# A hybrid encoder block on one core: the right-hand SBUF pools begin 96 bytes lower

## The chip, the cores and the metric

The kernel runs on one core of one Trainium2 chip. The metric is the device time in microseconds of one execution. Three runs of the kernel before took 1058.28, 1058.58 and 1059.94 us; the median is 1058.58 us. A profile of one execution goes with it.

## The reference

The reference is one encoder block over T = 1040 positions (16 meta tokens put ahead of 1024) of 1024 channels, in float32.

```python
u = _rms_norm(h, pre_w)
z = u @ w_in                       # ten parts: 1024 x 7680
# branch A: bidirectional retention, 4 heads (dk 128, dv 256), chunks of 128
o_r = group_norm(retention_fwd + retention_bwd) * ret_nw * silu(rg)
y_r = o_r @ w_rb
# branch B: attention within +-128, 8 query heads, 2 key groups, meta keys, a sink logit
o_a = windowed_sink_attention(aq, ak, av, sink) * silu(ag)
y_a = o_a @ w_ab
mix = sigmoid(gr) * y_r + sigmoid(ga) * y_a
return h + _rms_norm(mix @ w_o, post_w)
```

(The middle lines are shortened; rotary positions and the decay tables are left out here.)

## The kernel before

The products need more than one rounded pass. Each operand is split into a high part (a copy rounded to the matmul's type, on ScalarE or GpSimd) and a low part (the difference, on VectorE, L89 to L90), and `mm3` (L72 to L78) issues three matmuls for one product of tiles:

```python
nc.tensor.matmul(o, ah, bh, start=first, stop=False, **kw)   # L74
nc.tensor.matmul(o, al, bh, start=False, stop=False, **kw)   # L75
latest[:] = [nc.tensor.matmul(o, ah, bl, start=False, stop=last, **kw).ins]   # L76
```

The second argument is the stationary operand, which a weight load brings into the array (128 x 128); the third is the moving operand, which is streamed past it (256 to 512 columns). Each matmul has its own weight load.

Tiles live in pools. A pool on the left grows up from the low end of each partition, one with `side="right"` grows down from the high end. The right-hand pools are `wp` (L46: the split weights `wh` and `wl` of a unit of 256 columns, and the packed meta tokens `xm`), `aw` (L1331: split queries `aqh` and `aql`, the raw scores) and, when these two are closed (L1529), `lp` (L1530: split blocks `lh` and `ll`, six of each, raw weights, staging tiles). The left-hand ones that matter are `keep` (L44: `big`, the split input in four tiles of 4 x 1040 columns, and small vectors such as `nsink`, `dtab`, `rcol`, `rbc`, `rnw`, `mhalf`, L93 to L99), `ra`, `rp`, `va`, `ap` (retention and attention) and `yt` (L1546: the tiles T2, T3 and T4).

The built program shows where the tiles begin in each partition. The right-hand pools end at byte 229,344; `wp` begins at 194,528 and `lp` at 172,000, both 224 modulo 256. Every stationary tile in them has rows of 512 bytes or a multiple, so all of them begin at 224 modulo 256. In `big` a row of 1040 columns is 4160 bytes, so each step of the contraction index k moves the address by 64 bytes modulo 256: the slices pass through 0, 64, 128 and 192. The slices of T in `yt` all begin at 64 modulo 256, the retention's split tiles in `rp` and `va` at 192.

The work has three stages.

- Projections, retention and attention (0 to about 560 us). `proj` (L135) makes transposed projections: the stationary operand is a weight from `wp`, the moving one a slice of `big` (256, 272 or 512 columns). `projT` (L155) makes the values (`pv`, `pav`) the other way round: the stationary operand is a slice of `big`, the moving one 256 columns of `wp`. Retention (L440) multiplies tiles of `rp` with tiles of `rp`; attention (L1337) takes its queries from `aw`. Projections of the next head fill the gaps of retention and attention in a hand-written order.
- The gates and the two branch projections (to about 975 us), and the output projection (to the end). They are done in 2 x 2 blocks with seven products in place of eight (`Phase`, L931 on). `product` (L987) issues four `mm3` per product: the stationary operand is `lh` or `ll` from `lp`, the moving one 512 columns of `big` or T. Blocks are prepared six products ahead (`LEAD`, L1080).

The order of the instructions on each engine comes from this hand-written order and a scheduler.

Of the kernel before, what the change touches and what calls it, by code (L numbers as in the profile page):

```python
# [7 lines left out]
F32 = mybir.dt.float32  # L8
# [8 lines left out]
P = 128  # L17
# [21 lines left out]
def block_kernel(ctx: ExitStack, tc: tile.TileContext, x0, xT, x, meta, w_in, w_rb, w_ab, w_out, post_w,  # L39
# [2 lines left out]
    PSUM = bass.MemoryType.PSUM  # L42

    keep = ctx.enter_context(tc.tile_pool(name="keep", bufs=1))  # L44
    w_stack = ExitStack()
    wp = w_stack.enter_context(tc.tile_pool(name="wp", bufs=1, side="right"))  # L46
    ps = ctx.enter_context(tc.tile_pool(name="ps", bufs=1, reuse_waits="tile", space=PSUM))
# [43 lines left out]


    vec = keep.tile([P, 2 * KT], F32, name="vec")  # L93
    nsink = keep.tile([P, 8], F32, name="nsink")
    dtab = keep.tile([P, 28], F32, name="dtab")
    rcol = keep.tile([P, 9], F32, name="rcol")
    rbc = keep.tile([P, T], F32, name="rbc")
    rnw = keep.tile([P, KT], F32, name="rnw")
    mhalf = keep.tile([P, 16], F32, name="mhalf")  # L99
    nc.vector.memset(mhalf, -0.5)  # L100

    def fetch_w(src, u):
# [163 lines left out]
    with tc.tile_pool(name="setup", bufs=1, reuse_waits="tile") as st:  # L266
# [89 lines left out]
        for c in range(9):  # L356
            a, b = cols(c)
            t = st.tile([P, D if c < 7 else T], F32, tag="xn" if c < 7 else "xr", bufs=7 if c < 7 else KT - 1,
                        name=f"xn{c}")[:, 0:D]
# [1271 lines left out]
```

## Time and profile before

| what | value |
|---|---|
| median of three runs | 1058.58 us (1058.28 to 1059.94) |
| span of the profiled execution | 1057.8 us |
| TensorE busy | 1047.6 us, 99% |
| weight loads | 906.6 us, 86%, beside the matmuls |
| VectorE busy | 839.3 us, 79% |
| ScalarE busy | 507.2 us, 48% |
| GpSimd busy | 229.0 us, 22% |
| granted TensorE clock | 0.999 of full speed |
| read from and written to HBM | 124.32 MB and 57.68 MB |

A row of a group of instructions gives the source line, the engine, what is written from what, the shape, the count, and then busy time in us, the mean duration in ns, and the engine's idle time before it. The duration of a matmul overlaps that of the next one, since matmuls are pipelined; what counts for the time is the distance from one start to the next, and that is read from the timeline, whose rows begin with the start in us. A row of waits gives the engine that waited, the line, what it waited for, the total in us, how often, and the longest. A row of windows gives the stretch, its length, each engine's busy time with its count, PEclk, the DMA share and GB/s; with a filter, it gives PE's alone.

### The profile page before, as it was taken

How to read it: one execution, taken by the hardware profiler on the slowest of the kernel's cores; microseconds unless marked ns; L12 is line 12 of the kernel's file. 1: busy time of each engine (PE TensorE's matmuls, PEld its weight loads, DVE VectorE, ACT ScalarE, POOL GpSimd, SP SyncE). 2: the span in 40 equal slices, each digit the busy share in tenths (PEclk: the TensorE clock that was granted, in tenths of full speed). 3: DMA queues.
4: the chain of work that ended last, by engine and by line, in shares of the span. 5: the costliest groups of instructions: out<-in, count | busy, mean ns of one | idle time of the engine just before them, and what ended most of it. 6: DMA issues, size and time to landing. Idle time of an engine off the chain costs nothing. (4 is left out here: it accounts for less than half of the span.)

```text
span 1057.8 us, 17223 instructions
## 1 busy us (share of the span) xinstructions
PE 1047.6 (99%) x5880; PEld 906.6 (86%) x5880; DVE 839.3 (79%) x1788; ACT 507.2 (48%) x1127; POOL 229.0 (22%) x338
## 2 busy tenths in 40 slices
PE   9999999999999999999999999999999999999997
PEld 8998999989989888988888888787888888788886
DVE  7876758768875777778769988998799799778665
ACT  5531422523524566655667554455556446334432
POOL 3345244243242332444310000000000000111032
PEclk9999999999999999999999999999999999999999
DMA  9433222242231466665549679999925746789463
GB/s 352 168 86 86 70 42 80 71 98 89 84 83 61 101 181 192 165 181 159 165 155 338 201 254 321 302 309 353 387 94 168 250 159 232 225 226 317 119 120 79
DMA packets 96758, 188.43 MB, mean 178 GB/s; under 512 B 10944, under 2 KB 35552, under 8 KB 95856
## 3 DMA queue, kind: packets, MB, share of 16 engines
q1 hardware_dynamic: 79120, 162.89, 45.6%
q0 software_dynamic: 10176, 14.73, 9.2%
q10 hardware_dynamic: 7376, 9.73, 2.6%
q8 instruction: 46, 0.75, 0.3%
q14 instruction: 40, 0.33, 0.1%
HBM read 124.32 MB, written 57.68 MB: 172 GB/s over the span
## 5 line engine op out<-in xcount | busy, mean ns | idle before, releaser
L1246 POOL DMA_DIRECT2D mx_d<-c1a x4 | 3.6, 891 | 401.6 <-DVE c1a L1237 382.4
L75 PE MATMUL bz<-T,llz 128*128 128x512 f32 x192 | 75.9, 395 | 0.0
L76 PE MATMUL bz<-T,lhz 128*128 128x512 f32 x192 | 75.7, 394 | 0.0
L74 PE MATMUL bz<-T,lhz 128*128 128x512 f32 x192 | 75.6, 396 | 0.0
L74 PE MATMUL pv<-wh,big 128*128 128x256 f32 x256 | 73.3, 286 | 0.0
L75 PE MATMUL pv<-wh,big 128*128 128x256 f32 x256 | 73.3, 286 | 0.0
L76 PE MATMUL pv<-wl,big 128*128 128x256 f32 x256 | 73.2, 286 | 0.0
L75 PE MATMUL bz<-big,llz 128*128 128x512 f32 x176 | 69.6, 395 | 0.2 <-DVE llz L90 0.2
L76 PE MATMUL bz<-big,lhz 128*128 128x512 f32 x176 | 69.5, 395 | 0.0
L74 PE MATMUL bz<-big,lhz 128*128 128x512 f32 x176 | 68.7, 395 | 0.5 <-ACT lhz L942 0.5
L1377 ACT ACTIVATE p<-raw,nm 128x401 f32<-128x401 f32 (+1 forms) x64 | 38.4, 601 | 33.7 <-DVE nm L1374 32.4
L1387 POOL TENSOR_SCALAR p<-p,den 128x400 f32<-128x400 f32 (+1 forms) x60 | 37.8, 687 | 68.2 <-DVE den L1380 64.1
L74 PE MATMUL paq<-big,wh 128*128 128x512 f32 x128 | 51.8, 405 | 0.0
L75 PE MATMUL paq<-big,wl 128*128 128x512 f32 x128 | 50.7, 396 | 0.0
L76 PE MATMUL paq<-big,wh 128*128 128x512 f32 x128 | 50.5, 395 | 0.0
L75 PEld LDWEIGHTS pv<-wh,big 128*128 128x128 f32 x256 | 48.3, 189 | 0.4
L74 PEld LDWEIGHTS pv<-wh,big 128*128 128x128 f32 x256 | 48.2, 188 | 0.4
L76 PEld LDWEIGHTS pv<-wl,big 128*128 128x128 f32 x256 | 48.3, 189 | 0.3
L76 PEld LDWEIGHTS bz<-T,lhz 128*128 128x128 f32 x192 | 36.0, 188 | 8.9
L75 PEld LDWEIGHTS bz<-T,llz 128*128 128x128 f32 x192 | 36.0, 188 | 8.8 <-DVE llz L90 0.3
L74 PEld LDWEIGHTS bz<-T,lhz 128*128 128x128 f32 x192 | 36.0, 188 | 8.7
L90 DVE TENSOR_TENSOR wl<-wr,wh 128x1024 fp32r<-128x1024 f32 x28 | 34.8, 1247 | 10.8 <-POOL wh L87 6.7
(616 smaller groups left out, 3613.6 us busy)
## 6 DMA issues: line engine op xcount, KB each, us to landing
wrz<-in_w_in_dram SPq DMA_DIRECT2D x32, 512.0 KB, 6.2
wr<-in_w_in_dram SPq DMA_DIRECT2D x29, 512.0 KB, 4.0
we<-in_w_in_dram SPq DMA_DIRECT2D x16, 512.0 KB, 4.2
tg<-tg_d SPq DMA_DIRECT2D x32, 256.0 KB, 5.0
T<-preT SPq DMA_DIRECT2D x6, 1024.0 KB, 8.2
e<-e ACTq DMA_DIRECT2D x20, 256.0 KB, 2.6
e<-e SPq DMA_DIRECT2D x20, 256.0 KB, 4.6
xn<-in_x_dram SPq DMA_DIRECT2D x8, 512.0 KB, 9.2
```

Of the source, the lines that this page charges most:

```text
L74: nc.tensor.matmul(o, ah, bh, start=first, stop=False, **kw)
L75: nc.tensor.matmul(o, al, bh, start=False, stop=False, **kw)
L76: latest[:] = [nc.tensor.matmul(o, ah, bl, start=False, stop=last, **kw).ins]
L90: return nc.vector.tensor_tensor(o, i, hi.bitcast(F32), ALU.subtract).ins
L1246: nc.gpsimd.dma_start(d, to, accum_op=ALU.add)
L1377: last["exp"] = nc.scalar.activation(p[:, 0:1 + wid], raw[e_][:, 0:1 + wid], AF.Exp, scale=-1.0, bias=nm_[:, e_:e_ + 1], accum_out=den[:, ...
L1387: nc.gpsimd.tensor_scalar(pt[e_][:, 0:wid], pt[e_][:, 0:wid], den[:, e_:e_ + 1], 1.0, op0=ALU.mult, op1=ALU.mult)
```

## The change

A pool `edge` is opened on the right ahead of `wp`, with one tile of 24 columns (96 bytes), of which 8 hold `nsink`, formerly in `keep`. `mhalf` grows from 16 to 24 columns, so that `keep` has the size it had.

```diff
     keep = ctx.enter_context(tc.tile_pool(name="keep", bufs=1))
+    edge = ctx.enter_context(tc.tile_pool(name="edge", bufs=1, side="right"))
     w_stack = ExitStack()
     wp = w_stack.enter_context(tc.tile_pool(name="wp", bufs=1, side="right"))
...
-    nsink = keep.tile([P, 8], F32, name="nsink")
+    nsink = edge.tile([P, 24], F32, name="nsink")[:, 0:8]
     dtab = keep.tile([P, 28], F32, name="dtab")
     rcol = keep.tile([P, 9], F32, name="rcol")
     rbc = keep.tile([P, T], F32, name="rbc")
     rnw = keep.tile([P, KT], F32, name="rnw")
-    mhalf = keep.tile([P, 16], F32, name="mhalf")
+    mhalf = keep.tile([P, 24], F32, name="mhalf")
     nc.vector.memset(mhalf, -0.5)
```

In the built program every tile of `wp`, `aw` and `lp` begins 96 bytes lower: 128 modulo 256 in place of 224. `dtab`, `rcol`, `rbc`, `rnw` and `mhalf` begin 32 bytes lower. All other tiles stay. Source lines from L45 on are one higher in the kernel after.

## The prediction

> **What bounds the kernel now.** I read the page's first part, then the engine's waits, then a table by window, and last the timeline of single matmuls.
>
> ```profile
> span 1057.8 us, 17223 instructions
> PE 1047.6 (99%) x5880; PEld 906.6 (86%) x5880; DVE 839.3 (79%) x1788; ACT 507.2 (48%) x1127; POOL 229.0 (22%) x338
> ```
>
> TensorE is busy for all but 10.2 us of the span. The waits of PE alone:
>
> ```profile
> PE idle L309 <- DVE warm L207: 1.5, 1, 1.5
> PE bz L74 <- ACT lhz L942: 0.5, 1, 0.5
> PE pt L1404 <- POOL p L1387: 0.5, 2, 0.3
> PE pt L1404 <- DVE pal L90: 0.4, 1, 0.4
> PE pt L1409 <- DVE pbl L90: 0.3, 1, 0.3
> PE bz L75 <- DVE llz L90: 0.2, 1, 0.2
> ```
>
> Together 3.4 us. So the time is the sum of the distances from one matmul's start to the next, plus a start and a tail that the edit does not lengthen. The windows say that the clock is not a variable here:
>
> ```profile
> 100.00:200.00 100.00, 100.00 (x778) 95.97 (x777) 74.71 (x212) 34.52 (x106) 36.22 (x56) 1.00 0.24 64
> 800.00:900.00 100.00, 100.00 (x431) 80.49 (x430) 92.75 (x154) 53.66 (x97) 0.00 (x0) 1.00 0.64 213
> ```
>
> PEclk is 1.00 in both, and between 800 and 900 us 431 matmuls fill 100 us, 232 ns each. A change of addresses can only matter by moving that distance. How many matmuls read an operand from the moved side? The windows filtered by tile, over the whole span, first for matmuls that read T, then for those that read big:
>
> ```profile
> 0.00:1057.80 1057.80, 244.29 (x1020) 1.00 0.58 178
> 0.00:1057.80 1057.80, 679.21 (x3456) 1.00 0.58 178
> ```
>
> These 4476 of 5880 matmuls, 923.5 us of busy time, each pair one left-hand operand (T or big) with one right-hand operand. I therefore watch 0.2% of the whole, 2.1 us: that is about 0.5 ns per matmul of this group, and about what a measurement of this kernel can tell from no change.
>
> **What the change does to the instructions.** From the two built programs: all five queues hold the same instructions in the same order with the same waits; only the memset of mhalf is wider. Every tile of wp, aw and lp begins 96 bytes lower, so 224 modulo 256 becomes 128; five small tiles of keep begin 32 bytes lower; nothing else moves. So no wait is added, removed or passed, and no DMA is issued anywhere else.
>
> The memset:
>
> ```profile
> 0.80 0.07 DVE L100 MEMSET mhalf<- 128x16 f32 x1 [0.80 <-PEq L1621]
> 1.37 0.06 DVE L207 MEMSET warm<- 128x1 f32 x1
> ```
>
> 16 columns take 70 ns and 1 column 60, so 8 more columns cost about 5 ns, ahead of the first matmul's 1.5 us wait: +0.005 us, on the path, nothing.
>
> The other engines read and write moved tiles as well. A subtraction that touches lp alone or with keep, one that reads left tiles and writes keep's big, and one that writes yt:
>
> ```profile
> L90 DVE TENSOR_TENSOR llz<-wrz,lhz 128x512 fp32r<-128x512 f32 x36 | 24.4, 692 | 4.3 <-ACT lhz L942 4.2
> L90 DVE TENSOR_TENSOR big<-z,big 128x512 fp32r<-128x512 f32 x16 | 10.9, 694 | 0.0
> L90 DVE TENSOR_TENSOR T<-xT,T 128x512 fp32r<-128x512 f32 x12 | 7.7, 688 | 0.0
> ```
>
> Tiles at 224 (llz, lhz), at 0, 64, 128 and 192 (big, 4160-byte rows, so each k begins 64 bytes further) and at 64 (T) take 688 to 694 ns. I cost VectorE's and ScalarE's work at no change. The cover, if they did move, is the 3.4 us of waits above: PE hardly ever waits for them. DMAs go to the same tiles at other offsets; no PE wait in the list names one, so I cost them at nothing too.
>
> **The weight loads.** Four kinds of stationary operand: big at all four phases against a right-hand moving operand (pv), lhz at 224 against T at 64, val in ra at 192, vh in rp at 192 (the last two not on the right):
>
> ```profile
> L74 PEld LDWEIGHTS pv<-wh,big 128*128 128x128 f32 x256 | 48.2, 188 | 0.4
> L74 PEld LDWEIGHTS bz<-T,lhz 128*128 128x128 f32 x192 | 36.0, 188 | 8.7
> L75 PEld LDWEIGHTS po<-pah,val 128*128 128x128 f32 x64 | 12.1, 189 | 1.1
> L74 PEld LDWEIGHTS pa<-vh,sh 128*128 128x128 f32 x32 | 6.0, 189 | 0.3
> ```
>
> 188 to 189 ns whether the tile begins at 224, 192, or one of 0, 64, 128, 192. big already serves as stationary operand at 128 for a quarter of its loads and is no cheaper. So a stationary address of 128 modulo 256 buys nothing in the load by itself: bound 0 to 1 ns per load, and it lies beside the running matmul.
>
> **The distance between matmuls.** This is the term with something in it. First and last of 60 starts that stream T, of 70 that stream big, of 48 pv, and of 12 in a row with both operands in rp:
>
> ```profile
> 641.82 0.39 PE L74 MATMUL bz<-T,lhz 128*128 128x512 f32 x1
> 655.82 0.39 PE L74 MATMUL bz<-big,lhz 128*128 128x512 f32 x1
> ...
> 889.22 0.39 PE L74 MATMUL br<-big,lhr 128*128 128x512 f32 x1
> 905.50 0.40 PE L74 MATMUL ba<-T,lha 128*128 128x512 f32 x1
> ...
> 36.91 0.28 PE L75 MATMUL pv<-wh,big 128*128 128x256 f32 x1
> 42.56 0.28 PE L75 MATMUL pv<-wh,big 128*128 128x256 f32 x1
> ...
> 214.36 0.28 PE L74 MATMUL pa<-vh,sh 128*128 128x256 f32 x1
> 215.79 0.28 PE L76 MATMUL pk<-big,wh 128*128 128x256 f32 x1
> ```
>
> - T: 14.00 us / 60 = 233.3 ns. Both addresses are fixed modulo 256: moving 64, stationary 224.
> - big: 16.28 / 70 = 232.6 ns. Stationary 224, moving walking through four phases.
> - pv: 5.65 / 48 = 117.7 ns. Moving 224, stationary walking through four phases.
> - rp: 1.43 / 12 = 119.2 ns. Both at 192, the same stretch of columns as pv.
>
> So the distance depends on the pair of addresses, but little: 0.7 ns of 233 (0.3%) and 1.5 ns of 118 (1.3%). Where one operand walks, all four differences are passed through, and it is a little quicker; where the pair is fixed, it is a little slower. After the change big still walks through four differences, now multiples of 64 bytes in place of odd multiples of 32, and T has one fixed pair again (64 against 128). An average over four evenly spaced differences should stay where it is; the fixed pair may stay at 233.3 or fall to the walking 232.6. The value I take for big is 0, bounds below; for T, between 0 and 0.7 ns on 996 matmuls (0.7 us), I take half, -0.3 us. (The 996 are the 1020 of the windows row less the 24 half-width ones of the last product.)
>
> **Sum.** 1057.8 us span + 0.005 (memset) + 0 (other engines) + 0 (loads) + 0 (big) - 0.3 (T) = 1057.5 us. The runs' median, 1058.58 us, lies 0.8 us above the span of the profiled execution, which I keep: 1058.3 us.
>
> **Rivals.**
>
> - *Slower: the aligned pace.* The only stretches in which both operands stand on one 64-byte grid without a right-hand tile are those like rp's, and they are the slow ones, 119.2 against 117.7. If the pace is set by whether the two reads stand on the same 64-byte grid, the change moves every pair of big onto it. Price: of big's 3456 matmuls 1920 are 512 wide and 1536 are 256 or 272 wide (counted from the program's shapes). 1536 x 1.5 ns = 2.3 us; 1920 x 0.7 ns (the slow fixed pair of T against big) = 1.3 us; T stays. +3.6 us, so 1062.2. It decides as soon as pv's distance is above 118.5 ns. For it: two rows, both slow with fixed pairs. Against it: T is slow at an odd multiple of 32, so the grid is not what makes it slow; having a fixed pair is.
> - *Faster: the misaligned right side is what costs.* If 32 bytes off the grid costs the 0.7 ns that T shows, everything on the right loses it: 4476 x 0.7 ns = 3.1 us, so 1055.5. For it: T, at 224 against 64, is the slowest 512-wide class. Against it: rp's stretch, on the grid on both sides, is slower than pv's.
> - *Much faster: the reads collide, and the collision goes.* From 256 to 512 columns the distance grows by 232.6 - 117.7 = 114.9 ns, which leaves 117.7 - 114.9 = 2.8 ns per matmul that does not grow with the columns. If that remainder is two reads meeting, and it goes, 4476 x 2.8 ns = 12.5 us: 1046. Against it: the remainder is there for all phases seen. [...]
> - *The change doesn't reach the chip's addresses.* The built program has them moved, so this has no chance of its own.
>
> **How the numbers follow.** No difference that counts: 0.43, 1058.3 us. The aligned pace and whatever else is slower: 0.31, near 1062. The misaligned cost: 0.22, near 1055.5; the collision: 0.04, near 1046. Faster 0.26, same 0.43, slower 0.31. The likeliest case's own range is 1056.5 to 1060.7. The range of 8 in 10 reaches over the slow rival with half its price again (3.6 x 1.5 = 5.4 us, 1064) and over the fast one with half again (3.1 x 1.5 = 4.7, 1053.6), and leaves the collision out: 1053.5 to 1064.
>
> **What would show it.** If I am right, PE keeps 99%, LDWEIGHTS stays at 188 to 189 ns in all four groups, the stretches give 232 to 234 ns and 117 to 119 ns, and VectorE's subtractions stay at 688 to 694 ns. The slow rival shows as pv at 119 and over; the fast one as T near 232.6 and big near 232; the collision as both below 230. A longer weight load, or a PE wait over 2 us on a DMA or on VectorE, would show that I priced the wrong thing.

## The result, and the profile after

The changed kernel takes 1057.30 us (median of 21 runs, 1055.90 to 1059.00); the kernel before, measured with it, 1058.78 us (21 runs). The ratio is 0.9986, with a 95% interval of 0.9979 to 0.9992: about 1.5 us less, clear of noise and inside the 0.2% that the prediction called no difference (the interval just reaches past it).

The page of the kernel after:

```profile
span 1055.5 us, 17223 instructions
PE 1045.0 (99%) x5880; PEld 904.4 (86%) x5880; DVE 838.7 (79%) x1788; ACT 506.4 (48%) x1127; POOL 228.4 (22%) x338
```

PE is as full as before, and its busy time fell by 2.6 us, the span by 2.3. Source lines are one higher. The weight loads with big and with lhz as stationary operand, and VectorE's subtraction in lp:

```profile
L75 PEld LDWEIGHTS pv<-wh,big 128*128 128x128 f32 x256 | 48.2, 188 | 0.4
L75 PEld LDWEIGHTS bz<-T,lhz 128*128 128x128 f32 x192 | 35.9, 187 | 8.8
```

```profile
L91 DVE TENSOR_TENSOR llz<-wrz,lhz 128x512 fp32r<-128x512 f32 x36 | 24.3, 688 | 4.0 <-ACT lhz L943 3.8
```

187 to 188 ns and 688 ns, where it was 188 and 692: the weight loads and VectorE are not where the time went. The waits of PE sum to 3.3 us (before 3.4), though not all at the same places: one of 0.4 us for `pal` in attention is gone, and one of 0.6 us for `big` near the start is new. The windows filtered by tile, T and then big:

```profile
0.00:1057.80 1057.80, 244.33 (x1020) 1.00 0.58 178
0.00:1057.80 1057.80, 676.74 (x3456) 1.00 0.58 178
```

T stands at 244.33 us (before 244.29). big fell from 679.21 to 676.74 us, 2.5 us over 3456 matmuls. The same stretches of instructions in the kernel before, first 70 starts that stream big out of lp, then the 256-wide matmuls with T in the last product:

```profile
810.89 0.39 PE L74 MATMUL bz<-big,lhz 128*128 128x512 f32 x1
827.19 0.40 PE L74 MATMUL br<-T,lhr 128*128 128x512 f32 x1
...
1048.20 0.28 PE L74 MATMUL bo<-T,lho 128*128 128x256 f32 x1
1050.96 0.28 PE L76 MATMUL bo<-T,lho 128*128 128x256 f32 x1
```

And in the kernel after, with the 60 starts that stream T ahead of them:

```profile
639.45 0.39 PE L75 MATMUL bz<-T,lhz 128*128 128x512 f32 x1
653.45 0.39 PE L75 MATMUL bz<-big,lhz 128*128 128x512 f32 x1
...
808.78 0.39 PE L75 MATMUL bz<-big,lhz 128*128 128x512 f32 x1
825.00 0.40 PE L75 MATMUL br<-T,lhr 128*128 128x512 f32 x1
...
1045.83 0.28 PE L75 MATMUL bo<-T,lho 128*128 128x256 f32 x1
1048.45 0.28 PE L77 MATMUL bo<-T,lho 128*128 128x256 f32 x1
```

T: 14.00 us / 60 = 233.3 ns, as before. big: 16.30 / 70 = 232.9 ns before, 16.22 / 70 = 231.7 after. T 256 wide: 2.76 / 23 = 120.0 ns before, 2.62 / 23 = 113.9 after, with the same matmuls in the same order.

The prediction named other stretches as well. These are its 70 starts of big in the kernel after, with the longest distance among them, and its 48 starts of pv:

```profile
887.04 0.39 PE L75 MATMUL br<-big,lhr 128*128 128x512 f32 x1
...
900.71 0.48 PE L76 MATMUL ba<-big,lla 128*128 128x512 f32 x1
901.03 0.39 PE L77 MATMUL ba<-big,lha 128*128 128x512 f32 x1
...
903.34 0.40 PE L75 MATMUL ba<-T,lha 128*128 128x512 f32 x1
...
36.53 0.28 PE L76 MATMUL pv<-wh,big 128*128 128x256 f32 x1
42.19 0.28 PE L76 MATMUL pv<-wh,big 128*128 128x256 f32 x1
```

This stretch of big takes 16.30 us, 232.9 ns a matmul, and no less than before (16.28). One distance in it is 0.32 us; without that one the other 69 take 231.6 ns each. pv takes 5.66 / 48 = 117.9 ns, before 117.7. So a single stretch says little, and the change is better read from all of them. The next table has the mean distance of each kind of matmul to the next, over all those that have neighbours of their own kind on both sides, and without the few distances over 250 ns (over 130 ns for the narrow ones):

| matmuls | count | before, ns | after, ns |
|---|---|---|---|
| big out of `lp`, 512 wide | 1104 | 232.53 | 231.96 |
| big out of `wp`, 512 wide | 816 | 232.82 | 232.37 |
| pv and pav, 256 wide | 960 | 118.37 | 118.09 |
| big out of `wp`, 256 wide | 432 | 118.34 | 117.53 |
| big out of `wp`, 272 wide | 144 | 125.23 | 125.62 |
| T, 512 wide | 996 | 233.40 | 233.34 |

Times the counts, the rows of big make 1.6 us, T's wide ones 0.06 and its narrow ones 0.14: together 1.8, near the 1.5 us of the runs. So the time went where only an address moved.

### The profile page after: what moved, and what is told of

Its sections match the earlier page's. It is cut to its first block, busy times and chain, and to the rows that moved or that the text cites. A ratio compares the mean times of both kernels' runs of the same rounds, so it can differ in the third digit from the quotient of the medians.

```text
span 1055.5 us, 17223 instructions
## 1 busy us (share of the span) xinstructions
PE 1045.0 (99%) x5880; PEld 904.4 (86%) x5880; DVE 838.7 (79%) x1788; ACT 506.4 (48%) x1127; POOL 228.4 (22%) x338
## 5 line engine op out<-in xcount | busy, mean ns | idle before, releaser
L76 PE MATMUL bz<-T,llz 128*128 128x512 f32 x192 | 75.8, 395 | 0.2 <-DVE llz L91 0.2
L75 PE MATMUL bz<-T,lhz 128*128 128x512 f32 x192 | 75.2, 394 | 0.0
L76 PE MATMUL pv<-wh,big 128*128 128x256 f32 x256 | 73.2, 286 | 0.0
L75 PE MATMUL pv<-wh,big 128*128 128x256 f32 x256 | 73.2, 286 | 0.0
L76 PE MATMUL bz<-big,llz 128*128 128x512 f32 x176 | 69.5, 395 | 0.1
L75 PE MATMUL bz<-big,lhz 128*128 128x512 f32 x176 | 68.5, 394 | 0.5 <-ACT lhz L943 0.5
L75 PE MATMUL paq<-big,wh 128*128 128x512 f32 x128 | 51.7, 404 | 0.0
L76 PE MATMUL paq<-big,wl 128*128 128x512 f32 x128 | 50.7, 396 | 0.0
L76 PEld LDWEIGHTS pv<-wh,big 128*128 128x128 f32 x256 | 48.2, 188 | 0.4
L75 PEld LDWEIGHTS pv<-wh,big 128*128 128x128 f32 x256 | 48.2, 188 | 0.4
L76 PEld LDWEIGHTS bz<-T,llz 128*128 128x128 f32 x192 | 35.9, 187 | 9.5 <-DVE llz L91 0.7
L75 PEld LDWEIGHTS bz<-T,lhz 128*128 128x128 f32 x192 | 35.9, 187 | 8.8
```

## The experiments

In these texts the difference is the address of the stationary operand minus that of the moving one, modulo 256 bytes. Before it is 160 for T; in the changed kernel it is 64. A pair is held when both addresses stay the same modulo 256 from one matmul to the next; an operand walks when its address steps by 64 bytes, as big's does. Theory A, B and so on are those of the expectation above each result.

### Bare streams: what a pair of addresses costs

Every stream is 48 matmuls; this is the inner part, with S as stationary and M as moving tile, i the stationary phase in steps of 32 bytes, m the moving phase (16 is 64 bytes, 48 is 192):

```diff
+    def stream(name, n, pairs):
+        t = ps.tile([P, 512], F32, tag="o", name=name)
+        for i, (st, mv) in enumerate(pairs):
+            nc.tensor.matmul(t[:, 0:n], st, mv, start=i == 0, stop=i == len(pairs) - 1)
...
+    for w, n in (("n", 256), ("w", 512)):
+        for f, m in (("f", 16), ("g", 48)):
+            for i, ph in enumerate("abcdefgh"):
...
+                    p += mm3(st(8 * i, k % 4, 0), st(8 * i, k % 4, 1), fixed(m, n, k % 4, 0), fixed(m, n, k % 4, 1))
+                stream(w + f + ph, n, p)
```

> This kernel leaves out the whole block and copies x to the output; it runs bare streams of 48 matmuls with a weight load each, in the hi/lo order of mm3, for every stationary phase 0, 32, ..., 224 modulo 256: with a moving operand fixed at 64 and at 192, with one that walks by 64 bytes per k as in big, 256 and 512 columns wide, and with the stationary operand walking (as in pv). Theory A (the pace is a function of the difference stationary minus moving modulo 256): the streams at moving 64 and at moving 192 agree where the differences agree; difference 160 gives 120.0 ns at 256 columns and 233.3 ns at 512, difference 64 gives 113.9 ns and 233.3 ns, difference 0 gives 119 to 120 ns; walking streams lie between 231 and 234 ns and between 117 and 119 ns at all phases. Theory B (only the 64-byte grid matters): stationary phases 0, 64, 128, 192 agree with each other, and so do 32, 96, 160, 224, in every kind of stream. [...]

The timeline of PE, one row a stream (start, length, then the stream as the written tile; n is 256 columns and w 512, f a moving phase of 64 and g of 192, a to h the stationary phase 0 to 224):

```profile
39.70 5.91 PE L44 MATMUL nfc<-M,S 128*128 128x256 f32 x48
45.45 5.84 PE L44 MATMUL nfd<-M,S 128*128 128x256 f32 x48
51.12 5.82 PE L44 MATMUL nfe<-M,S 128*128 128x256 f32 x48
56.78 5.79 PE L44 MATMUL nff<-M,S 128*128 128x256 f32 x48
...
187.19 11.08 PE L44 MATMUL wfc<-M,S 128*128 128x512 f32 x48
198.12 11.35 PE L44 MATMUL wfd<-M,S 128*128 128x512 f32 x48
209.31 11.36 PE L44 MATMUL wfe<-M,S 128*128 128x512 f32 x48
220.51 11.40 PE L44 MATMUL wff<-M,S 128*128 128x512 f32 x48
231.74 11.32 PE L44 MATMUL wfg<-M,S 128*128 128x512 f32 x48
...
321.09 11.05 PE L44 MATMUL wgg<-M,S 128*128 128x512 f32 x48
331.98 11.35 PE L44 MATMUL wgh<-M,S 128*128 128x512 f32 x48
```

Start to next start, by 48: at 256 columns difference 0 (nfc) takes 5.75 / 48 = 119.8 ns, difference 64 (nfe) 5.66 / 48 = 117.9. At 512 columns difference 0 takes 227.7 (wfc) and 226.9 (wgg, at other phases of both), 64 (wfe) 233.3, 96 (wff) 234.0. Over the last 24 starts of each stream, after the run-in, the held streams give:

| difference | 0 | 32 | 64 | 96 | 128 | 160 | 192 | 224 |
|---|---|---|---|---|---|---|---|---|
| 256 columns, moving at 64 | 120.0 | 118.3 | 117.8 | 117.5 | 118.8 | 120.0 | 117.8 | 117.8 |
| 256 columns, moving at 192 | 119.8 | 118.3 | 117.8 | 117.3 | 118.6 | 120.0 | 117.8 | 117.8 |
| 512 columns, moving at 64 | 226.7 | 233.3 | 233.3 | 234.5 | 232.7 | 233.3 | 233.3 | 233.3 |
| 512 columns, moving at 192 | 226.7 | 233.3 | 233.3 | 234.4 | 232.7 | 233.3 | 228.9 | 233.3 |

The two moving phases agree at every difference but one (192 at 512 columns: 233.3 and 228.9). Theory A holds for held pairs and B falls: differences 0 and 64, both on the 64-byte grid, take 226.7 and 233.3 ns at 512 columns. Where the moving operand walks as big does, B holds instead: the last 24 starts give 231.7 ns at all four multiples of 64 and 232.2 to 232.3 at all four odd multiples of 32 (512 columns), 118.3 against 118.9 to 119.0 (256 columns). Where the stationary operand walks, as in pv, it is the other way round: the last 24 starts give 118.3 ns at the multiples of 64 and 117.8 at the odd multiples of 32. In the kernel pv and pav do not follow that (118.4 before, 118.1 after); why is open. The kernel's T, 256 wide, falls out too: 113.9 ns at difference 64, where the bare stream gives 117.8; why is open as well.

### One part alone: wp and aw, then lp, then T

```diff
     w_stack = ExitStack()
+    edge = w_stack.enter_context(tc.tile_pool(name="edge", bufs=1, side="right"))
     wp = w_stack.enter_context(tc.tile_pool(name="wp", bufs=1, side="right"))
```

> The 96 bytes only while wp and aw are open: lp begins at 224 again. Theory A: matmuls against wp and aw keep what they gained between the two profiles (512 wide against big 0.9 us, pv and pav 0.4 us, scores from aw 0.7 us), lp's streams go back; in all about 1.2 us faster than before, the T stretches of 256 columns back at 120 ns. Rival (the 1.5 us come from the small tiles of keep or from something outside the streams): no part of it belongs to wp and aw, the sum of clean distances in wp's streams stays as before within 0.2 us.

1057.69 us, ratio 0.9991 (0.9982 to 1.0000): 0.9 us of the 1.5, at the edge of what can be told, and less than the 1.2 expected. The trace says more than the time. `wp`'s streams have the changed kernel's means (512 wide 232.34 ns, pv and pav 118.07, 256 wide 117.53), while big out of `lp` (232.53) and T's narrow ones (120.0) are those of the kernel before. The scores from `aw` did not gain the 0.7 us expected: with the same addresses as in the changed kernel, PE waits 0.6 us for `pal` right behind one of them, as it waits 0.4 us in the kernel before and not at all in the changed one. That part of the difference between the two profiles was a wait and not an address.

```diff
     w_stack.close()
+    edge = ctx.enter_context(tc.tile_pool(name="edge", bufs=1, side="right"))
+    edge.tile([P, 24], F32, name="unused")
     lp = ctx.enter_context(tc.tile_pool(name="lp", bufs=1, reuse_waits="tile", side="right"))
```

> The 96 bytes only for lp, after wp and aw are closed; keep is untouched. Theory A: 512-wide matmuls of lp against big go from 232.4 to 231.8 ns (0.6 us), T's 512-wide stay at 233.3, T's 256-wide go from 120 to 114 ns (0.14 us): 0.3 to 0.8 us faster than before. Rival (the small tiles of keep): nothing, within 0.2 us.

1058.09 us, ratio 0.9997 (0.9988 to 1.0006): not told from none. In its trace the stretch of 70 from before (808.73 us on) takes 231.8 ns as in the changed kernel and the 256-wide T 113.8. Big out of `lp` has the changed kernel's mean (231.96), `wp`'s streams have that of the kernel before (232.81, 118.37 and 118.32): each part moves with its own pool. As for the times, together with wp_only's 0.0009 the two ratios make 0.0012 of the 0.0014, each uncertain by 0.0009. keep's small tiles stayed where they were here, so they are not the cause of lp's part.

```diff
     yp, gp, yt = (ctx.enter_context(tc.tile_pool(name=n, bufs=1, reuse_waits="tile")) for n in ("yp", "gp", "yt"))
+    yt.tile([P, 24], F32, name="unused")
```

> Nothing on the right moves; the T tiles alone begin 96 bytes higher (160 modulo 256), so that the difference to lp's 224 is 64, as in the changed kernel. Theory A (the difference counts): T's 256-wide distances 114 ns, its 512-wide 233.3; big's streams as before. Rival (the stationary phase itself counts): T's 256-wide stay at 120 ns, since the stationary operand still begins at 224.

A single execution, 1059.98 us, from which the time is not told. T at 256 columns:

```profile
1048.30 0.28 PE L74 MATMUL bo<-T,lho 128*128 128x256 f32 x1
1050.91 0.28 PE L76 MATMUL bo<-T,lho 128*128 128x256 f32 x1
```

2.61 / 23 = 113.5 ns with lp at 224. The kernel before has the same stationary phase, and it takes 120.0 there; it has the moving phase of the changed kernel too, which takes 113.9. So the difference decides, and neither phase alone.

### Other offsets

The same edit as the change with another width of nsink's tile (40, 16 and 8 columns), and T's tiles alone moved by 160 bytes.

```diff
-    nsink = edge.tile([P, 24], F32, name="nsink")[:, 0:8]
+    nsink = edge.tile([P, 40], F32, name="nsink")[:, 0:8]
```

> The change with 160 bytes in place of 96: the right side begins at 64 modulo 256, so T (64) has difference 0 and big walks through multiples of 64. Theory A (the difference counts; bare streams give 226.7 ns at difference 0 and 512 columns, 233.3 at most others): T's 996 matmuls lose 6.6 ns each, 6.6 us, and the rest gains as in the changed kernel, 1.5 us: 1050.5 us. Rival 1 (the 64-byte grid alone counts): as the changed kernel, 1057.3 us, T at 233.3. Rival 2 (the state of 226.7 ns needs long unbroken streams, and T's come in runs of 12 to 60): T between 228 and 233, 1052 to 1057 us.

> Nothing on the right moves; the T tiles alone begin 160 bytes higher, at 224, so that T's difference is 0. Theory A: T's 512-wide distance falls from 233.3 to 226.7 ns, everything else stays: 6.6 us less than before, 1052 us; T's 256-wide go to 120 ns. Rival 1 (grid alone, or the stationary phase alone): no change, 1058.7 us.

> The change with 64 bytes: the right side begins at 160, an odd multiple of 32 as before, and T's difference is 96. Theory A: T at 234.4 ns (1.0 us more than before), big and the projections as before (232.2 to 232.5 ns walking): 1059.5 us. Rival 1 (the 64-byte grid alone counts): as before, 1058.7 us, T at 233.3. Rival (moving the small tiles of keep by 32 bytes made the gain): 1057.3 us.

> The change with 32 bytes: the right side begins at 192, a multiple of 64, and T's difference is 128. Theory A: T at 232.7 ns (0.7 us less), big and the projections as in the changed kernel (231.7 to 231.8 ns, 1.5 us less): 1056.5 us. Rival 1 (the grid alone counts): 1057.3 us with T at 233.3.

The 60 starts of T (the same instructions as above), in the kernel with 160 bytes on the right:

```profile
638.46 0.40 PE L75 MATMUL bz<-T,lhz 128*128 128x512 f32 x1
652.07 0.40 PE L75 MATMUL bz<-big,lhz 128*128 128x512 f32 x1
```

With T moved by 160:

```profile
640.41 0.39 PE L74 MATMUL bz<-T,lhz 128*128 128x512 f32 x1
654.05 0.40 PE L74 MATMUL bz<-big,lhz 128*128 128x512 f32 x1
```

With 64 bytes on the right:

```profile
641.76 0.39 PE L75 MATMUL bz<-T,lhz 128*128 128x512 f32 x1
655.82 0.39 PE L75 MATMUL bz<-big,lhz 128*128 128x512 f32 x1
```

With 32 bytes on the right:

```profile
640.53 0.39 PE L75 MATMUL bz<-T,lhz 128*128 128x512 f32 x1
654.48 0.39 PE L75 MATMUL bz<-big,lhz 128*128 128x512 f32 x1
```

| kernel | T's difference | bare stream | T in the kernel | time | ratio (95%) |
|---|---|---|---|---|---|
| 160 on the right | 0 | 226.7 | 13.61 / 60 = 226.8 | 1053.76 us | 0.9948 (0.9934 to 0.9962) |
| T by 160 | 0 | 226.7 | 13.64 / 60 = 227.3 | 1055.09 us | 0.9960 (0.9946 to 0.9974) |
| 64 on the right | 96 | 234.4 | 14.06 / 60 = 234.3 | 1060.05 us | 1.0011 (1.0002 to 1.0020) |
| 32 on the right | 128 | 232.7 | 13.95 / 60 = 232.5 | 1057.48 us | 0.9986 (0.9977 to 0.9995) |

Each of the four differences gives the pace of the bare stream, and the signs of the times follow: the edit with 64 bytes makes the kernel slower, that with 160 makes it 0.5% faster, the quickest here. With 64 bytes keep's small tiles lie as in the changed kernel and the time is longer than before; big out of `lp` (232.45 ns), pv and pav (118.42) and the 256-wide ones out of `wp` (118.31) stay near the means of before, so the small tiles did not make these gains. The 512-wide ones out of `wp` are an exception: they are at 232.44 off the 64-byte grid too. Whether their 0.4 us come from the grid, the small tiles or something else in the addresses is not shown. Three sizes were off. T by 160 gained 3.9 us where 6.6 were expected, and 160 on the right 5.2 where 8.1 were. 32 on the right gained 1.5 where some 2.2 were: the time is that of its rival (1057.3), and T's pace alone speaks against the rival. The windows filtered by tile of the kernel with 160 on the right, T and then big:

```profile
0.00:1057.80 1057.80, 238.67 (x1020) 1.00 0.59 178
0.00:1057.80 1057.80, 678.56 (x3456) 1.00 0.59 178
```

T lost 5.6 us, not 6.6: many runs of T have only 12 matmuls, and a stream takes some to settle. With 160 on the right the first three distances of a run are 230.0 ns on the mean, the next three 227.4, and from the seventh on it is 226.7 to 226.8; with T moved by 160 they are 232.8, 230.3, 229.0 by threes, and 226.7 from the tenth on. To that extent Rival 2 was right. big kept 0.65 us of the 2.5 that it gained with 96 bytes. What is lost lies in big out of `lp`, 232.7 ns on the mean where the changed kernel has 232.0; out of `wp` it is 232.3. Why its walk is slower here, on multiples of 64 as well, is open.

### Difference 0 for everything out of lp

```diff
-            h, l = (lp.tile([P, 4, P], R, tag=t, bufs=LEAD, name=f"{t}{self.nm}{u}_{p}") for t in ("lh", "ll"))
+            h, l = (lp.tile([P, 4, P + 16], R, tag=t, bufs=LEAD, name=f"{t}{self.nm}{u}_{p}")[:, :, 0:P] for t in ("lh", "ll"))
...
-    LEAD = 6
+    LEAD = 5
...
+    yt.tile([P, 16], F32, name="unused")
-        B[n] = [yt.tile([P, 4, 512], R, name=f"{n}{s}")[:, :, :] for s in range(2)]
+        B[n] = [yt.tile([P, 4, 528], R, name=f"{n}{s}")[:, :, 0:512] for s in range(2)]
```

> The changed kernel, with a row of 144 columns in place of 128 in lh and ll and of 528 in place of 512 in T, T begun 64 bytes higher, and blocks prepared five products ahead in place of six (for the room): every 512-wide matmul out of lp now has difference 0 between its own two operands, big's too. Theory A, own pair: big falls from 231.8 to 226.7 ns (5.6 us) and T from 233.3 to 227.3 (6.0 us) against the changed kernel: 1046 us, less what five ahead costs. Theory A, next pair (the load that runs beside a matmul is that of the next one, so that one distance in three has difference 64): T and big both between 227 and 233 ns, 1047 to 1057 us. Rival (a gain needs a pair that is fixed in both addresses, not in their difference): T and big at 231.7 ns as the walking streams, 1056 us.

> The changed kernel with blocks prepared five products ahead in place of six, nothing else: the control for lp_zero. If five ahead costs nothing: 1057.3 us, waits of PE as before. If it costs, PE's waits for ScalarE and VectorE (lh, ll) grow, and lp_zero bears the same.

lead5 takes 1060.98 us, ratio to before 1.0024 (1.0015 to 1.0033), lp_zero 1060.09 us, 1.0010 (1.0001 to 1.0019). Five ahead costs 3.7 us against the changed kernel's 1057.30; two of the waits of lead5's PE that the changed kernel does not have:

```profile
PE br L75 <- ACT u3r L1025: 0.7, 1, 0.7
PE bz L75 <- ACT u3z L1025: 0.7, 1, 0.7
```

Against lead5, lp_zero gains some 0.9 us by the medians (0.0014 by the ratios, 1.5 us), not 11. The 60 starts of T in lp_zero:

```profile
639.90 0.40 PE L75 MATMUL bz<-T,lhz 128*128 128x512 f32 x1
653.82 0.39 PE L75 MATMUL bz<-big,lhz 128*128 128x512 f32 x1
```

13.92 / 60 = 232.0 ns, where a held pair at difference 0 gives 226.7. Over all its streams T takes 231.5 ns and big 231.5. So an own difference of 0 is not enough when both operands walk; both come near the rival's 231.7, and its 1056 us with lead5's 3.7 on top are near the time measured. The next pair's 227 to 233 ns take in the same paces, so it is not excluded here. That the load beside a matmul is that of the next one stands in the timeline of the kernel before: in a run of T the load for L76 and the matmul of L75 both start at 644.85 us, and the matmul of L76 at 645.09.

The third kernel of this set gives wh and wl rows of 272 columns in the same way (and cuts xm and the eight idle matmuls to 48 columns per k).

```diff
-            h, l = (wp.tile([P, 4, 256], R, tag=f"w{x}", bufs=4, name=f"w{x}{u}_{len(hi)}") for x in "hl")
+            h, l = (wp.tile([P, 4, 272], R, tag=f"w{x}", bufs=4, name=f"w{x}{u}_{len(hi)}")[:, :, 0:256] for x in "hl")
```

> lp_zero, and wh and wl with rows of 272 columns in place of 256 (xm is cut to 48 columns per k, the eight idle matmuls ahead to 384 columns): every 512-wide matmul out of wp has difference 0 too, but so have pv, pav, pk and pak, 256 wide. Theory A (256 wide, difference 0 is the slow one: 119.8 to 120.0 ns in bare streams against 117.8 to 118.3 walking): 816 x 5.6 ns = 4.6 us gained, 960 x 1.7 + 432 x 1.8 ns = 2.4 us lost against lp_zero, net 2 us faster. Rival (difference 0 is quick at all widths): 6 us faster than lp_zero.

1060.00 us, ratio 1.0011 (1.0002 to 1.0020): the same as lp_zero. Neither the 2 us nor the 6 came.

### Which pair counts when both walk

```diff
+    def pair(step, d, n, i):
+        s, m = 16 * ((step * i + d) % 4) + 192 * (i % 6), 16 * (step * i % 4) + 640 * (i % 6)
+        return S[:, s:s + 128], M[:, m:m + n]
```

> This kernel leaves out the whole block too and copies x to the output; streams of 48 matmuls at 256 and 512 columns in which both operands step by 0, 64, 128 or 192 bytes modulo 256 from one matmul to the next, so that the own difference (stationary minus moving of the same matmul) is held at 0, 64, 128 or 192 while the difference of the next stationary operand to the running moving one is own plus step. Held values from the first bare streams at 512 columns: 226.7 at 0, 233.3 at 64, 232.7 at 128, 228.9 or 233.3 at 192. Theory own pair: 226.7 ns wherever the own difference is 0, whatever the step. Theory next pair (the weight load that runs beside a matmul is that of the next): 226.7 wherever own plus step is 0 modulo 256, and 233.3, 232.7 or 233.3 at own difference 0 with step 64, 128, 192. Theory both must stand still: 226.7 only at step 0; everything else 231 to 233 ns. At 256 columns the same with 120.0 at 0, 117.8 at 64 and 192, 118.7 at 128.

Rows as above; u, v and x are steps of 64, 128 and 192 bytes, a to d an own difference of 0, 64, 128 and 192:

```profile
162.06 11.14 PE L44 MATMUL wua<-M,S 128*128 128x512 f32 x48
173.04 11.23 PE L44 MATMUL wub<-M,S 128*128 128x512 f32 x48
...
195.26 11.28 PE L44 MATMUL wud<-M,S 128*128 128x512 f32 x48
206.38 11.13 PE L44 MATMUL wva<-M,S 128*128 128x512 f32 x48
...
228.39 11.21 PE L44 MATMUL wvc<-M,S 128*128 128x512 f32 x48
239.43 11.36 PE L44 MATMUL wvd<-M,S 128*128 128x512 f32 x48
250.63 11.29 PE L44 MATMUL wxa<-M,S 128*128 128x512 f32 x48
261.76 11.35 PE L44 MATMUL wxb<-M,S 128*128 128x512 f32 x48
272.94 11.28 PE L44 MATMUL wxc<-M,S 128*128 128x512 f32 x48
```

Own difference 0: 10.98 / 48 = 228.8 ns at step 64 (wua), 11.13 / 48 = 231.9 at step 192 (wxa). Next difference 0: 231.7 (wud), 230.0 (wvc), 232.9 (wxb). The first two theories fall: own pair 0 is quick at one step and not at another, and next pair 0 never reaches 226.7. Of the third one half holds, 226.7 came only at step 0; the other half, 231 to 233 ns for all else, does not (228.8, 230.0). What rule holds when both operands walk stays open.

## Why the prediction was right, and where it was not

**Right: where the time is.** The change lies in the distance between starts; order, weight loads and VectorE stand as they did, and the waits sum to 3.3 us for 3.4. The forecast of no difference over 0.2% holds, and with it the signs named for it: PE at 99%, weight loads at 187 to 189 ns, pv at 117.9, T at 233.3. That it holds is in part luck: the 0.2% was set by what can be told in a measurement, the time fell by 1.5 of these 2.1 us, and it fell in the term that was put at 0.

**Mis-sized: big, "the value I take is 0".** It measured -2.5 us in the profiled pair, and -1.6 us by the means above, which leave the waits out. The step that failed is "an average over four evenly spaced differences should stay where it is". The bare streams with a walking moving operand show that it does not: 231.7 ns on multiples of 64, 232.2 on odd multiples of 32, which is 1.0 us on 1920 matmuls.

**Mis-sized: T, -0.3 us.** It measured 0: 14.00 us for 60 before and after. Differences 160 and 64 happen to cost the same at 512 columns (233.3 both in the bare streams). The 0.14 us that 23 narrow matmuls gained (2.76 - 2.62) was not foreseen.

**Mis-sized: the time outside the span, 0.8 us.** Runs that list both show 2.0 us (1057.46 against a span of 1055.5). So the profiled execution of before took about 1059.8 us, near the top of its kernel's range (1057.40 to 1059.94), and the comparison of the two profiles (2.3 us) overstates the 1.5 us of the runs.

**The slow rival (one 64-byte grid is slow)** read rp's 119.2 ns as the price of the grid. rp's pairs, both at 192, have difference 0, and difference 0 held at 256 columns takes 119.8 to 120.0 in the bare stream. In the bare streams with a walking moving operand the grid is the quicker way (231.7 ns against 232.2 to 232.3 at 512 columns, 118.3 against 118.9 to 119.0 at 256). Its sign, pv at 119 and over, did not come.

**The fast rival (32 bytes off the grid costs)** had the sign right, and big's 512-wide matmuls did gain about the 0.5 ns that it named as big near 232. It was wrong for T, on which it was built. For pv's side the kernel's means agree with it (118.4 to 118.1) and the bare streams do not (117.8 off the grid, 118.3 on it).

**The collision.** Relief of this kind exists, but at a difference that the change holds in no stream of 512 columns: 226.7 ns at difference 0. The bare streams take 226.7 to 234.5 ns for the same held 512-column matmul by the two addresses alone. That the two reads meet was the author's inference from this dependence on addresses; no run shows it.

## What to carry to other kernels

When TensorE is full (99% here) and streams 256 to 512 float32 columns against a fresh weight load each, try the offset between the stationary and the moving tiles modulo 256 bytes: here a pad of 160 bytes was worth 0.5% and one of 64 cost 0.1%. Measure it with bare streams in the kernel's own order and width, since the best difference at 512 columns (0, 226.7 ns) is among the worst at 256 (119.8 to 120.0 in a range of 117.3 to 120.0). Then measure the kernel itself: for held pairs of 512 columns the bare streams gave the pace within 0.6 ns, for pv (118.4 before and 118.1 after, 117.8 and 118.3 in the streams), for narrow T (113.9 and 117.8) and where both operands walk (231.5 in lp_zero, 226.7 for the held pair) they did not. Read distances between starts, not durations, over many stretches and not one, and check the time outside the span from runs that list both before a profile's span is set against a median.

## What the runs showed of the hardware

- In run pace a held pair of addresses settles, over the last 24 of 48 starts, into a pace that goes by the difference modulo 256 bytes: 226.7, 228.9, 232.7, 233.3 or 234.5 ns at 512 columns, 117.3 to 120.0 at 256. One difference (192) showed two paces at 512 columns, 233.3 (moving at 64) and 228.9 (moving at 192), so the difference alone does not say all; whether it is the phases or the way in is open.
- When both operands step by 128 bytes (run pace2), 256 columns take 116.7 ns at all four own differences (5.60 us from each stream's start to the next, by 48), less than any held pair of the bare streams.
- None of this shows in the weight load's own duration (187 to 189 ns in every group shown of the kernels before and after).
